# Blocks of the v table three ahead of their sums, and a store and a load of expert weights in two, in a two-layer PEER network

## The chip, the cores and the metric

The kernel runs on one core of one Trainium2 chip. What counts is the device time in microseconds (us) of one execution. The core has five engines with queues of instructions of their own: TensorE (PE; PEld is its weight load), VectorE (DVE), ScalarE (ACT), GpSimd (POOL) and SyncE (SP). SP issues most of the transfers, ACT the stores of two intermediate results, POOL the indirect gathers; 16 DMA engines carry them all.

## The reference, cut to what matters

The network has two layers. In each, three mixers (a state-space scan, differential attention, neighbourhood attention) are merged, and then comes a mixture of 16384 experts, each of which is one row of a table u and one row of a table v. For every token 8 heads choose 16 experts each:

```python
def peer_ffn(h, wq, subkeys, u_tab, v_tab):
    ...
        q = (hb @ wq).reshape(bn, PEER_CHUNK, PEER_HEADS, 2, PEER_DHALF)
        s = jnp.einsum('bchxd,hxnd->bchxn', q, subkeys).astype(jnp.float32)
        sv, si = lax.top_k(s, PEER_TOPK)
        ...
        eidx = jnp.take_along_axis(cidx, pos, axis=-1)
        g = jax.nn.softmax(best, axis=-1).astype(hb.dtype)
        act = jax.nn.gelu(jnp.einsum('bchkd,bcd->bchk', u_tab[eidx], hb))
        return jnp.einsum('bchk,bchkd->bcd', g * act, v_tab[eidx])
```

There are 512 tokens of 1024 channels and 256 context tokens; the last layer needs the tokens alone. All is float32.

## The kernel before, in words

The change lies in the expert part. The kernel computes it in two ways side by side. For some tokens (two tiles of 128 in layer 0, one in layer 1) it gathers the chosen rows of u and v: `gathered` lets POOL fetch 128 rows of 4 KB at a time into one of 5 buffers `grow` (512 KB), and DVE works each off (L1234 for u, L1242 for v). For the others (n = 512 tokens in layer 0, 384 in layer 1) it computes all 16384 experts densely, in 128 blocks of 128 experts, and multiplies each with a weight that is zero for an expert that wasn't chosen.

The dense way has two stages. In the **early stage** `early` multiplies the u blocks with the tokens, and ACT stores the activations of each block in DRAM (`actd`, L1258 and L1259). Meanwhile `route` finds the chosen experts and makes the weight tables: for each token group of 32 tokens PE sums a table `gst` (128 x 128 experts x 32 tokens, 2 MB), ACT evicts it (L1190) and stores it in DRAM (`gd<-gst`, L1193). There are 16 token groups in layer 0 and 12 in layer 1; the last one is ready at the very end of the early stage. In layer 0 a part of the gathers of u is also still under way there: twelve rows of it stand on DVE behind the early stage's last work.

Then come the **sums**, in `experts`. `block(i)` brings a block's operands: every eighth block the weights of the next eight blocks for all token groups (`gt<-gd`, 2 MB in layer 0, 1.5 MB in layer 1), the block's activations (`act`, 256 or 192 KB), and the v table's block (`raw`, 512 KB). DVE multiplies w = act * gt (L1278). Products are made in three passes of a shorter format, so `split` cuts w into wh (ACT, L61) and wl (DVE, L62), and `chunk` cuts raw into hiv (ACT, L61) and lov (DVE, L62). `sums` issues the matmuls wh x hiv (L1288), wh x lov (L1289) and wl x hiv (L1291), which add up in PSUM over all blocks. The last 4 blocks (LAST) are all made first and then summed tile by tile. Beside the sums run the rest of the gathers and what finishes their tokens (`beside`).

The order on each engine is that in which the program writes its instructions, by generators that take turns; an engine goes through its queue in that order, and each instruction waits for its operands and for its buffer. The pools of the early stage are closed ahead of the sums, and the sums' pools lie in the same memory: the first tiles of the sums also wait until what lay there has been read or stored. Below, hi and lo belong to u blocks, hiv and lov to v blocks.

Of the kernel before, what the change touches and what calls it, by code (L numbers as in the profile page):

```python
# [50 lines left out]
class Net:  # L51
# [1044 lines left out]
    def route(self, l, sv, si, p, picks=None, at=None):  # L1096


        nc, v = self.nc, self.nc.vector
# [29 lines left out]
        def lookup(out, x, against, table, op):  # L1129
            for h in range(0, 8, 2):  # L1130
                sh = [128, 2, 16, 16]
                eq = p.tile(sh, F32, name="eq")
                v.tensor_tensor(eq, x[:, 16 * h:16 * h + 32].rearrange("p (h k) -> p h k", h=2).unsqueeze(3).to_broadcast(sh),
                                against[:, None, None, :].to_broadcast(sh), op=op)
                v.tensor_tensor(eq, eq, table[:, h:h + 2][:, :, None, :].to_broadcast(sh), op=ALU.mult)
                v.tensor_reduce(out[:, 16 * h:16 * h + 32].rearrange("p (h k) -> p h k", h=2), eq, axis=AX.X, op=ALU.add)
                yield 1.30
# [44 lines left out]
        def table(b, t0, st, oj, og, ol):  # L1182
            for q in range(0, 8, 4):
                ps = self.ps1("mm")
                for z in range(4):
                    o = ps[:, 128 * z:128 * z + 128]
                    a, y = divmod(q + z, 2)
                    nc.tensor.matmul(o, oj[:, a, :, y], og[:, a, :, y], start=True, stop=False)
                    nc.tensor.matmul(o, oj[:, a, :, y], ol[:, a, :, y], start=False, stop=True)
                nc.scalar.activation(st[:, :, t0 + q:t0 + q + 4].rearrange("p i t -> p t i"),  # L1190
                                     ps.rearrange("p (t i) -> p t i", t=4), AF.Copy, scale=1.0 / GSCALE)
            if t0 == 24:
                nc.scalar.dma_start(self.gd[l][at + b], st)  # L1193

        last = None
        for b in range(4):
            st = p.tile([128, 128, 32], F32, name="gst", tag="gst")
            for t0 in range(0, 32, 8):
                t = 32 * b + t0
                oi, oj, og = [p.tile(sh, F16, name=n, bufs=3) for n in ("oi", "oj", "og")]  # L1200
                v.tensor_tensor(oj, iota, over(ij[:, 1], t), op=ALU.is_equal)
                v.tensor_tensor(oi, iota, over(ij[:, 0], t), op=ALU.is_equal)
                v.tensor_tensor(og, oi, over(gh, t), op=ALU.mult)
                v.tensor_tensor(oi, oi, over(gl, t), op=ALU.mult)
                if last is not None:
                    table(*last)
                last = b, t0, st, oj, og, oi
                yield 2.40
        table(*last)

    def gathered(self, l, halves, rows, picks, p):
# [50 lines left out]
    def experts(self, l, n, p, ends, fill, cost):  # L1262


        nc, v = self.nc, self.nc.vector
        nh = n // 128
        stay = [self.ps2() for _ in range(nh)]
        parts = {}
        spent = 0.0

        def block(i):
            if i % 8 == 0:
                self.gt = p.tile([128, 4 * nh, 8, 32], F32, name="gt")
                self.dma(self.gt, self.gd[l][16 - 4 * nh:, :, i:i + 8].rearrange("b j i t -> j b i t"))
            act = p.tile([128, n], F32, name="act", bufs=3)
            self.dma(act, self.actd[l][i, :, :n])
            w = p.tile([128, n], F32, name="w")
            v.tensor_mul(w.rearrange("p (b t) -> p b t", t=32), act.rearrange("p (b t) -> p b t", t=32), self.gt[:, :, i % 8])  # L1278
            wh, wl = [p.tile([128, n], F32R, name=a, bufs=LAST + 2) for a in ("wh", "wl")]
            self.split(w, wh, wl)  # L1280
            parts[i] = (wh, wl, *self.chunk(self.a["peer_v"][l, i], "v"))

        def sums(i, x):
            ps, t = stay[x], slice(128 * x, 128 * x + 128)
            cs = [slice(512 * s, 512 * s + 512) for s in range(2)]
            wh, wl, vh, vl = parts[i]
            for c in cs:
                nc.tensor.matmul(ps[:, c], wh[:, t], vh[:, c], start=i == 0, stop=False)  # L1288
                nc.tensor.matmul(ps[:, c], wh[:, t], vl[:, c], start=False, stop=False)  # L1289
            for c in cs:  # L1290
                m = nc.tensor.matmul(ps[:, c], wl[:, t], vh[:, c], start=False, stop=i == 127)  # L1291
            return m

        marks = [None] * AHEAD
        for i in range(128 - LAST):
            block(i)
            for x in range(nh):
                m = sums(i, x)
            marks.append(m)
            self.pace = marks.pop(0)  # L1300
            while fill is not None and spent < cost * (i + 1) / (128 - LAST):
                c = next(fill, None)
                if c is None:
                    fill = None
                else:
                    spent += c
        for _ in fill or ():
            pass
        for i in range(128 - LAST, 128):
            block(i)  # L1310
        for x in range(nh):
            for i in range(128 - LAST, 128):
                sums(i, x)
            ends(x, stay[x])
# [273 lines left out]
```

## Time and profile before

| | |
|---|---|
| three runs | 4790.73, 4791.86, 4794.95 us (median 4791.86) |
| profiled execution: its own time | 4793.69 us |
| profiled execution: its span, first to last instruction | 4791.9 us |
| mean granted clock of PE, as a share of full speed | 0.961 |
| PE busy | 4438.4 us (93%) |
| DVE busy | 3780.0 us (79%) |
| ACT busy | 1858.3 us (39%) |
| POOL busy | 1129.2 us (24%) |
| moved by the DMA engines | 1209.93 MB, 252 GB/s over the span |

The profile is one execution. Its times count from the span's start. An engine is busy while it computes; issuing a transfer and waiting don't count. A granted clock (PEclk) of 1.00 is 2.4 GHz, one of 0.50 is 1.2 GHz. Behind an instruction of a timeline, square brackets name the idle time of its engine ahead of it and what released it; an engine's name with a q behind it (ACTq, SPq) is the issuing of a transfer. SP's transfers run on the queue q1, ACT's on q10, POOL's gathers on q0.

### The profile page before, as it was taken

What the parts mean: (1) busy time and instruction counts of PE and PEld (TensorE: products, weight loads), DVE (VectorE), ACT (ScalarE), POOL (GpSimd) and SP (SyncE); (2) the same over time, 40 slices, a digit from 0 to 9 for tenths busy, and PEclk for the clock granted to TensorE, in tenths of its full rate; (3) what the DMA queues carried; (4) which work ended last, traced back from release to release, by engine and by line L of the source; (5) the groups of instructions that cost most, each with busy time, mean ns of one, the idle gap of its engine ahead of it and who ended that gap; (6) DMA issues with size and microseconds to landing.
All of it is one profiled execution on the core that took longest, in us unless ns stands there. A gap on an engine that the chain in (4) does not pass through costs nothing. (4 is left out here: it accounts for less than half of the span.)

```text
span 4791.9 us, 68877 instructions
## 1 busy us (share of the span) xinstructions
PE 4438.4 (93%) x24197; PEld 3715.9 (78%) x24197; DVE 3780.0 (79%) x8710; ACT 1858.3 (39%) x3079; POOL 1129.2 (24%) x772
## 2 busy tenths in 40 slices
PE   8998998889989999879999997999889999989998
PEld 4787886677767778658888876877789899968887
DVE  8377985668888999987787763877555899968887
ACT  3244454443222445443222223445333355533333
POOL 0000000000555355534433300000000133325552
PEclk9999998899999999989999998999899999999999
DMA  7453435654899789999999945442444599999997
GB/s 245 152 146 103 145 119 173 222 185 148 305 337 322 246 320 341 348 352 378 358 343 352 344 175 171 142 142 89 166 149 138 191 333 356 341 331 381 377 375 260
DMA packets 461397, 1209.93 MB, mean 252 GB/s; under 512 B 47530, under 2 KB 181754, under 8 KB 457466
## 3 DMA queue, kind: packets, MB, share of 16 engines
q1 hardware_dynamic: 309562, 685.37, 42.0%
q0 software_dynamic: 110592, 402.70, 23.0%
q10 hardware_dynamic: 40896, 117.46, 6.3%
q8 instruction: 190, 3.11, 0.3%
q14 instruction: 157, 1.29, 0.1%
HBM read 1026.30 MB, written 179.04 MB: 252 GB/s over the span
## 5 line engine op out<-in xcount | busy, mean ns | idle before, releaser
L1220 POOL DMA_INDIRECT grow<-in_u_rows,pick x384 | 514.9, 1341 | 2900.1 <-DVE cand L1104 1179.5
L61 ACT CAST hi<-raw 128x1024 fp32r<-128x1024 f32 x490 | 513.0, 1052 | 876.1 <-PE s L71 602.2
L62 DVE TENSOR_TENSOR lo<-raw,hi 128x1024 fp32r<-128x1024 f32 x490 | 596.4, 1220 | 284.7 <-ACT hi L61 279.9
L72 PE MATMUL s<-h2h,lo 128*128 128x512 f32 (+1 forms) x2048 | 760.7, 372 | 49.6 <-DVE lo L62 49.2
L70 PE MATMUL s<-h2h,hi 128*128 128x512 f32 (+1 forms) x2048 | 769.7, 376 | 9.3 <-ACT eact L1258 9.0
L1220 POOL DMA_INDIRECT grow<-in_v_rows,pick x384 | 614.1, 1599 | 693.8 <-PE stay L1291 248.4
L71 PE MATMUL s<-h2l,hi 128*128 128x512 f32 (+1 forms) x2048 | 759.1, 371 | 0.0
L1288 PE MATMUL stay<-hiv,wh 128*128 128x512 f32 x1792 | 708.5, 396 | 47.5 <-ACT hiv L61 47.5
L1289 PE MATMUL stay<-lov,wh 128*128 128x512 f32 x1792 | 708.6, 395 | 0.0
L1242 DVE SCALAR_TENSOR_TENSOR row<-grow,gw,row 128x1024 f32<-128x1024 f32 x381 | 488.3, 1282 | 98.9 <-DMA grow<-in_v_rows,pick 95.8
L1291 PE MATMUL stay<-hiv,wl 128*128 128x512 f32 x1792 | 562.7, 395 | 0.0
L1234 DVE SCALAR_TENSOR_TENSOR grow<-grow,row 128x1024 f32<-128x1024 f32 x384 | 463.3, 1220 | 98.0 <-DMA grow<-in_u_rows,pick 92.4
L72 PEld LDWEIGHTS s<-h2h,lo 128*128 128x128 f32 x2048 | 389.8, 190 | 108.7 <-DVE lo L62 64.2
L61 ACT CAST wh<-w 128x512 fp32r<-128x512 f32 (+1 forms) x256 | 145.5, 569 | 773.3 <-DVE w L1278 369.5
L1288 PEld LDWEIGHTS stay<-hiv,wh 128*128 128x128 f32 x1792 | 338.5, 189 | 126.5 <-ACT hiv L61 47.9
L70 PEld LDWEIGHTS s<-h2h,hi 128*128 128x128 f32 x2048 | 390.4, 191 | 55.3 <-ACT eact L1258 13.4
L71 PEld LDWEIGHTS s<-h2l,hi 128*128 128x128 f32 x2048 | 390.3, 191 | 43.1
L1289 PEld LDWEIGHTS stay<-lov,wh 128*128 128x128 f32 x1792 | 338.4, 189 | 80.3 <-DVE lov L62 1.3
L1291 PEld LDWEIGHTS stay<-hiv,wl 128*128 128x128 f32 x1792 | 338.1, 189 | 78.9
L62 DVE TENSOR_TENSOR lov<-raw,hiv 128x1024 fp32r<-128x1024 f32 x256 | 312.4, 1220 | 6.5 <-ACT hiv L61 5.0
L61 ACT CAST hiv<-raw 128x1024 fp32r<-128x1024 f32 x256 | 268.3, 1049 | 64.1 <-DMA raw<-in_peer_v 62.2
L1278 DVE TENSOR_TENSOR w<-act,gt 128x512 f32<-128x512 f32 (+1 forms) x256 | 158.8, 621 | 102.9 <-DMA act<-actd 101.4
(424 smaller groups left out, 8759.6 us busy)
## 6 DMA issues: line engine op xcount, KB each, us to landing
raw<-in_peer_u SPq DMA_DIRECT2D x256, 512.0 KB
raw<-in_peer_v SPq DMA_DIRECT2D x256, 512.0 KB
gd<-gst ACTq DMA_DIRECT2D x28, 2048.0 KB
raw<-in_w_in SPq DMA_DIRECT2D x88, 512.0 KB
actd<-eact ACTq DMA_DIRECT2D x128, 256.0 KB
gt<-gd SPq DMA_DIRECT2D x16, 2048.0 KB
act<-actd SPq DMA_DIRECT2D x128, 256.0 KB
adaw<-in_ada_w SPq DMA_DIRECT2D x48, 512.0 KB
```

Of the source, the lines that this page charges most:

```text
L61: self.nc.scalar.copy(hi, x)
L62: self.nc.vector.tensor_sub(lo, x, hi.bitcast(F32))
L70: mm(ps, lh, rh, start=start and k == 0, stop=False)
L71: mm(ps, lh, rl, start=False, stop=False)
L72: mm(ps, ll, rh, start=False, stop=stop and k == n - 1)
L1220: d = nc.gpsimd.indirect_dma_start(out=t, out_offset=None, in_=self.a[table], in_offset=bass.IndirectOffsetOnAxis(ap=picks[y][0][:, j:j + ...
L1234: v.scalar_tensor_tensor(t, t, 1.0, h, op0=ALU.mult, op1=ALU.mult, accum_out=u[:, j:j + 1])
L1242: v.scalar_tensor_tensor(h, t, w[:, j:j + 1], h, op0=ALU.mult, op1=ALU.add)
L1278: v.tensor_mul(w.rearrange("p (b t) -> p b t", t=32), act.rearrange("p (b t) -> p b t", t=32), self.gt[:, :, i % 8])
L1288: nc.tensor.matmul(ps[:, c], wh[:, t], vh[:, c], start=i == 0, stop=False)
L1289: nc.tensor.matmul(ps[:, c], wh[:, t], vl[:, c], start=False, stop=False)
L1291: m = nc.tensor.matmul(ps[:, c], wl[:, t], vh[:, c], start=False, stop=i == 127)
```

## The change

Three things change, for both layers. The store of the last token group's table is cut at expert block 8: first the weights of the first 8 blocks (128 KB), then those of the other 120 (1.92 MB). The first load of gt is cut too: first all token groups but the last (15 in layer 0, 11 in layer 1), then the last one (128 KB). And the blocks of v are loaded and split three blocks ahead: those of blocks 0, 1 and 2 before the first block, and block i + 3's at the head of `block(i)`.

```diff
--- before.py
+++ after.py
@@ -1190,7 +1190,10 @@
                 nc.scalar.activation(st[:, :, t0 + q:t0 + q + 4].rearrange("p i t -> p t i"),
                                      ps.rearrange("p (t i) -> p t i", t=4), AF.Copy, scale=1.0 / GSCALE)
             if t0 == 24:
-                nc.scalar.dma_start(self.gd[l][at + b], st)
+
+                cuts = (0, 8, 128) if at + b == 15 else (0, 128)
+                for i, j in zip(cuts, cuts[1:]):
+                    nc.scalar.dma_start(self.gd[l][at + b, :, i:j], st[:, i:j])
 
         last = None
         for b in range(4):
@@ -1268,17 +1271,29 @@
         parts = {}
         spent = 0.0
 
+        def table(i):
+            if i < 128:
+                tables[i] = self.chunk(self.a["peer_v"][l, i], "v")
+
+
+        tables = {}
+        for i in range(3):
+            table(i)
+
         def block(i):
+            table(i + 3)
             if i % 8 == 0:
                 self.gt = p.tile([128, 4 * nh, 8, 32], F32, name="gt")
-                self.dma(self.gt, self.gd[l][16 - 4 * nh:, :, i:i + 8].rearrange("b j i t -> j b i t"))
+                cuts = (0, 4 * nh - 1, 4 * nh) if i == 0 else (0, 4 * nh)
+                for b, e in zip(cuts, cuts[1:]):
+                    self.dma(self.gt[:, b:e], self.gd[l][16 - 4 * nh + b:16 - 4 * nh + e, :, i:i + 8].rearrange("b j i t -> j b i t"))
             act = p.tile([128, n], F32, name="act", bufs=3)
             self.dma(act, self.actd[l][i, :, :n])
             w = p.tile([128, n], F32, name="w")
             v.tensor_mul(w.rearrange("p (b t) -> p b t", t=32), act.rearrange("p (b t) -> p b t", t=32), self.gt[:, :, i % 8])
             wh, wl = [p.tile([128, n], F32R, name=a, bufs=LAST + 2) for a in ("wh", "wl")]
             self.split(w, wh, wl)
-            parts[i] = (wh, wl, *self.chunk(self.a["peer_v"][l, i], "v"))
+            parts[i] = (wh, wl, *tables.pop(i))
 
         def sums(i, x):
             ps, t = stay[x], slice(128 * x, 128 * x + 128)
```

What this moves shows on three engines. In the rows that follow, brackets name what an instruction waits for: DMAHW (a transfer of SP's or ACT's, the digit is its semaphore), DMASW (a gather of POOL's), or an engine.

SP, beginning of layer 0's sums, before:

```order
L58 DMA raw<-in_peer_u 128x1024 [waits DMAHW4_49,DMAHW0_49,DVE_49]
L58 DMA raw<-in_peer_u 128x1024 [waits DMAHW7_49,DMAHW2_49,DVE_49]
L58 DMA gt<-gd_107 128x16x256 [waits DMAHW4_49,DMAHW3_49,DMAHW7_49,DVE_49,Activation_49]
L58 DMA act<-actd_109 128x512 [waits DMAHW5_49,Activation_49]
L58 DMA raw<-in_peer_v 128x1024 [waits DMAHW6_49,DMAHW1_49]
L58 DMA act<-actd_109 128x512
```

and with the change:

```order
L58 DMA raw<-in_peer_u 128x1024 [waits DMAHW4_49,DMAHW0_49,DVE_49]
L58 DMA raw<-in_peer_u 128x1024 [waits DMAHW7_49,DMAHW2_49,DVE_49]
L58 DMA raw<-in_peer_v 128x1024 [waits DMAHW5_49,DMAHW1_49,DVE_49]
L58 DMA raw<-in_peer_v 128x1024 [waits DMAHW6_49,DMAHW3_49,DVE_49]
L58 DMA raw<-in_peer_v 128x1024 [waits DMAHW7_49,DVE_49]
L58 DMA raw<-in_peer_v 128x1024 [waits DMAHW0_49,DVE_49]
L58 DMA gt<-gd_107 128x15x256 [waits DMAHW1_49,DMAHW3_49,DVE_49,Activation_49]
L58 DMA gt<-gd_107 128x256 [waits DMAHW3_49,DMAHW2_49]
L58 DMA act<-actd_109 128x512 [waits DMAHW4_49,Activation_49]
L58 DMA raw<-in_peer_v 128x1024
L58 DMA act<-actd_109 128x512 [waits DMAHW5_49]
```

Four loads of v and 15 groups of gt now stand ahead; the last group's load and the first act follow them.

DVE at the same place, before:

```order
L1234 SCALAR_TENSOR_TENSOR grow,gu<-grow,row_9271 128x1024 [waits DMASW3_49,DVE_49]
L1234 SCALAR_TENSOR_TENSOR grow,gu<-grow,row_9271 128x1024 [waits DMASW4_49,DVE_49]
L1234 SCALAR_TENSOR_TENSOR grow,gu<-grow,row_9271 128x1024 [waits DMASW5_49,DVE_49]
L1278 TENSOR_TENSOR w<-act,gt 128x512 [waits DMAHW4_49,DMAHW5_49,DMAHW3_49,Activation_49]
L62 TENSOR_TENSOR wl<-w,wh 128x512 [waits PE_49,Activation_49]
L1278 TENSOR_TENSOR w<-act,gt 128x512 [waits DMAHW7_49]
L62 TENSOR_TENSOR lov<-raw,hiv 128x1024 [waits DMAHW6_49,Activation_49]
```

and with the change (line numbers are 3 and 15 higher):

```order
L1237 SCALAR_TENSOR_TENSOR grow,gu<-grow,row_9271 128x1024 [waits DMASW3_49,DVE_49]
L1237 SCALAR_TENSOR_TENSOR grow,gu<-grow,row_9271 128x1024 [waits DMASW4_49,DVE_49]
L1237 SCALAR_TENSOR_TENSOR grow,gu<-grow,row_9271 128x1024 [waits DMASW5_49,DVE_49]
L62 TENSOR_TENSOR lov<-raw,hiv 128x1024 [waits DMAHW5_49,PE_49,Activation_49]
L62 TENSOR_TENSOR lov<-raw,hiv 128x1024 [waits DMAHW6_49,Activation_49]
L62 TENSOR_TENSOR lov<-raw,hiv 128x1024 [waits DMAHW7_49,Activation_49]
L62 TENSOR_TENSOR lov<-raw,hiv 128x1024 [waits DMAHW0_49,Activation_49]
L1293 TENSOR_TENSOR w<-act,gt 128x512 [waits DMAHW3_49,DMAHW4_49,DMAHW2_49,DMAHW1_49]
L62 TENSOR_TENSOR wl<-w,wh 128x512 [waits PE_49,Activation_49]
```

The rows of the gather stay ahead; four lov have come between the last of them and the first w.

ACT, beginning of layer 1's sums, before:

```order
L1259 DMA actd_110<-eact 128x384 [waits Activation_49]
L1190 ACTIVATE gst<-mm 128x4x128 [waits PE_49] x2
L1193 DMA gd_108<-gst 128x4096 [waits Activation_49]
L61 CAST wh<-w 128x384 [waits DMAHW1_49,DVE_49]
L61 CAST hiv<-raw 128x1024 [waits DMAHW4_49]
L61 CAST wh<-w 128x384 [waits DVE_49]
```

and with the change:

```order
L1262 DMA actd_110<-eact 128x384 [waits Activation_49]
L1190 ACTIVATE gst<-mm 128x4x128 [waits PE_49] x2
L1196 DMA gd_108<-gst 128x256 [waits Activation_49]
L1196 DMA gd_108<-gst 128x3840
L61 CAST hiv<-raw 128x1024 [waits DMAHW5_49,DVE_49]
L61 CAST hiv<-raw 128x1024 [waits DMAHW6_49,DVE_49]
L61 CAST hiv<-raw 128x1024 [waits DMAHW7_49,DVE_49]
L61 CAST hiv<-raw 128x1024 [waits DMAHW0_49]
L61 CAST wh<-w 128x384 [waits DMAHW4_49,DMAHW3_49,DVE_49]
L61 CAST hiv<-raw 128x1024 [waits DMAHW4_49]
```

The store is in two, and four casts hiv stand ahead of the first wh, which now waits for two transfers besides w.

## Rows read from the trace of the kernel before

**Rows 1.** The page, part 5: the sums' first matmul line.

```profile
L1288 PE MATMUL stay<-hiv,wh 128*128 128x512 f32 x1792 | 708.5, 396 | 47.5 <-ACT hiv L61 47.5
```

**Rows 2.** Windows over both stretches of sums: busy us of each engine.

```profile
2152.37:2862.00 709.63, 709.63 (x3050) 574.99 (x3051) 545.39 (x659) 204.32 (x262) 244.18 (x186) 1.00 0.91 329
4241.17:4778.90 537.73, 537.69 (x2304) 435.06 (x2304) 449.98 (x574) 191.76 (x261) 238.43 (x141) 1.00 0.97 357
```

**Rows 3.** Timeline of PE, both joints; in brackets the idle time before.

```profile
2125.37 0.22 PE L1189 MATMUL mm<-oi,oj 128*128 128x128 f16 x1
2152.37 1.65 PE L1288 MATMUL stay<-hiv,wh 128*128 128x512 f32 x3 [26.78 <-ACT hiv L61]
...
4220.19 0.22 PE L1189 MATMUL mm<-oi,oj 128*128 128x128 f16 x1
4241.17 1.22 PE L1288 MATMUL stay<-hiv,wh 128*128 128x512 f32 x2 [20.76 <-ACT hiv L61]
```

**Rows 4.** Timeline of ACT, joint of layer 1.

```profile
4222.31 0.33 ACTq L1193 DMA_DIRECT2D gd<-gst  x1
4239.43 0.51 ACT L61 CAST wh<-w 128x384 fp32r<-128x384 f32 x1 [17.14 <-DVE w L1278]
4240.07 1.05 ACT L61 CAST hiv<-raw 128x1024 fp32r<-128x1024 f32 x1
```

**Rows 5.** Timeline of SP, joint of layer 1.

```profile
4228.65 0.38 SPq L58 DMA_DIRECT2D gt<-gd  x1
```

**Rows 6.** Timeline of DVE, joint of layer 1.

```profile
4238.84 0.56 DVE L1278 TENSOR_TENSOR w<-act,gt 128x384 f32<-128x384 f32 x1 [21.26 <-DMA act<-actd]
```

**Rows 7.** Windows ahead of the two joints.

```profile
2099.00:2106.00 7.00, 6.39 (x50) 4.91 (x50) 7.00 (x12) 3.62 (x4) 3.46 (x4) 1.00 0.84 252
2106.00:2113.00 7.00, 6.50 (x39) 5.02 (x38) 7.00 (x13) 2.35 (x4) 3.45 (x3) 1.00 0.98 400
...
2120.00:2127.00 7.00, 5.59 (x36) 4.32 (x35) 7.00 (x12) 2.44 (x4) 4.82 (x3) 1.00 0.69 201
...
4216.00:4222.00 6.00, 4.41 (x36) 4.08 (x34) 1.57 (x4) 3.21 (x5) 0.00 (x0) 1.00 0.11 37
```

**Rows 8.** Timeline of DVE, its last instruction.

```profile
4786.89 1.23 DVE L1334 TENSOR_TENSOR raw<-raw 128x1024 f32<-128x1024 f32 x1
```

**Rows 9.** Timeline of DVE, beginning of layer 0's sums.

```profile
2152.61 1.22 DVE L62 TENSOR_TENSOR lov<-raw,hiv 128x1024 fp32r<-128x1024 f32 x1
2153.75 0.69 DVE L62 TENSOR_TENSOR wl<-w,wh 128x512 fp32r<-128x512 f32 x1
```

**Rows 10.** Timeline of ACT, joint of layer 0.

```profile
2127.18 0.33 ACTq L1193 DMA_DIRECT2D gd<-gst  x1
2150.75 0.62 ACT L61 CAST wh<-w 128x512 fp32r<-128x512 f32 x1 [23.60 <-DVE w L1278]
```

**Rows 11.** Timeline of SP, joint of layer 0.

```profile
2137.15 0.38 SPq L58 DMA_DIRECT2D gt<-gd  x1
```

**Rows 12.** Timeline of DVE, joint of layer 0.

```profile
2146.24 1.23 DVE L1234 SCALAR_TENSOR_TENSOR grow<-grow,row 128x1024 f32<-128x1024 f32 x1 [3.20 <-DMA grow<-in_u_rows,pick]
2150.02 0.69 DVE L1278 TENSOR_TENSOR w<-act,gt 128x512 f32<-128x512 f32 x1 [2.55 <-DMA act<-actd]
```

**Rows 13.** Windows inside the joint of layer 0.

```profile
2127.00:2137.00 10.00, 0.00 (x0) 0.00 (x0) 2.75 (x6) 0.15 (x1) 4.27 (x4) 0.60 0.99 375
2137.00:2150.00 13.00, 0.00 (x0) 0.00 (x0) 6.17 (x10) 0.00 (x0) 1.10 (x1) 0.50 1.04 382
```

**Rows 14.** DMA queues, 2127 to 2137, then 2137 to 2146.2.

```profile
q10 hardware_dynamic: 288, 2.36, 57.2%
q0 software_dynamic: 383, 1.39, 41.6%
...
q0 software_dynamic: 559, 2.01, 54.6%
q1 hardware_dynamic: 1480, 1.52, 48.8%
```

## The prediction

> **What bounds the kernel now.** I read the page's costliest groups first. PE is busy for 93% of the span, and the group that carries the expert sums has 47.5 us of idle time ahead of it, all of it put down to the cast hiv [rows 1]. Then the windows over both stretches of sums: PE is busy for 709.63 of 709.63 us in layer 0 and for 537.69 of 537.73 us in layer 1 [rows 2]. So inside a stretch nothing can be won, and the 47.5 us must lie ahead of them. The timeline of PE shows where: between the last matmul of the weight tables and the first of the sums it stands for 26.78 us in layer 0 and for 20.76 us in layer 1 [rows 3]. I call these two places the joints. What starts the sums earlier moves everything behind them by as much; the end of layer 0's sums leads into layer 1, and the last matmul (4778.90) into the tail. So the change is worth what it takes off the two joints.
>
> **Layer 1's joint, as it is.** ACT issues the store of the last weight table at 4222.31 [rows 4]. SP's gt load, which reads it back, goes at 4228.65 [rows 5]: the store took 6.34 us. The product w starts at 4238.84, after 21.26 us in which DVE had nothing else to do [rows 6]: gt and act took 10.2 us. Then come wh at 4239.43 and hiv at 4240.07 [rows 4], and PE at 4241.17 [rows 3].
>
> **What the change does there.** The last token group leaves in two stores, the first with the 8 first experts only (128 KB). The 11 groups stored long before are loaded without waiting for it, and so are v blocks 0 to 3: on SP they wait for buffers of the early stage only (first and third excerpt of the change). Ahead of this joint the DMA engines are busy for a share of 0.11 at 37 GB/s [rows 7], so these loads find room. What stays in the chain is: small store, small gt load, w, wh.
>
> - *Small store.* No row shows a 128 KB store. Above lies the line through two others: 2.1 MB in 6.34 us, and 0.52 MB of output in at most 3.8 us (DVE's last result at 4786.89 + 1.23 = 4788.12 [rows 8], span's end 4791.9). That is 1.6 us per MB, so at most 3.2 us for 0.13 MB. Below lie its bytes alone, 0.3 us. I take 2.0, a little over the middle, since the 0.52 MB row is the nearer one: it lands at 4224.3. The Trainium skill ("DMA: Bandwidth & Descriptors", Anatomy of one DMA) gives each DMA about 2.0 us of fixed time besides its bytes, which speaks against cutting; by it the small store would take an estimated 2.3 us, and the sum would be 0.3 us worse. No row here shows that fixed time by itself.
> - *gt and act loads.* At best 2 us, as the small store: 4226.3. At worst the 6.34 us of the whole store, which runs beside them, behind a small store of 3.2: 4231.9. I take 4230.1, near the upper end, because the 1.92 MB of the other store are under way until about 4229 (4222.7 + 6.34).
> - *wh* now lies where the old table lay, and waits for the second store too: 4229 to 4230. It costs nothing more if the loads come at 4230.1.
> - *v blocks.* Four casts hiv of 1.05 us [rows 4] fill ACT from 4223.0, and DVE makes four lov behind them, at a pitch of 1.14 (2153.75 less 2152.61 [rows 9]). They end at about 4228.6, just ahead of w: covered by the store. Without that cover they would add up to 4.56 us.
> - From w's start to wh 0.59, from there to wh's end 0.64 with the hand-over [rows 4, 6]: PE starts at 4230.1 + 1.2 = **4231.3, 9.8 us earlier**. Bounds: 4229.9 (four lov first, then w at 4228.6: -11.3) and 4233.1 (-8.0).
>
> **Layer 0's joint, as it is.** The store goes at 2127.18 [rows 10], gt's load at 2137.15 [rows 11]. This joint has other work: twelve rows of the gather wait on DVE, the last of which starts at 2146.24 after 3.20 us of waiting for its data, and w follows at 2150.02 [rows 12]. PE starts 6.13 us after that last gather landed. The DMA engines are full: share 0.99 at 375 GB/s, then 1.04 at 382 [rows 13].
>
> **What the change does there.**
> - *DVE's order.* Four lov now stand between the last gather row and w (the second excerpt of the change). From the landing: 1.23 for the gather row, 4 x 1.14 for the lov, 0.73 from w's start to wh and 0.62 for wh [rows 9, 10, 12]: 7.2 us instead of 6.13, **+1.07**. The casts hiv come from ACT, which has nothing else then (wh waited 23.60 us [rows 10]).
> - *The act load* still waits for the whole store, to about 2137.5; but 2 MB of gt no longer stand before it, so it lands before the gather does, and costs nothing.
> - *The last gather.* More bytes now ask for the engines before it: 2.1 MB of v, 2.1 of gt and 0.26 of act, 4.46 MB, where SP's queue had moved 1.52 MB from 2137 until the gather landed [rows 14]: 2.94 MB more. Room was there for 0.52 MB (one v block; 2099 to 2106, 252 GB/s) and (376 - 201) GB/s x 7 us = 1.22 MB (2120 to 2127) [rows 7]. The other 1.2 MB take 3.2 us at 376 GB/s. But the gathers have a queue of their own and hold about half of the engines' time beside the others: 41.6% to the store's 57.2%, then 54.6% to the loads' 48.8% [rows 14]. So about half of it comes first: 1.5 us. Ends: the gather lands right behind the one before it, whose row ended at 2143.1 (3.20 of waiting less 0.08 before the next could start: -3.1), or all 2.94 MB come ahead of it (+7.8).
> - Together **+2.5 us**, between -2.0 and +8.9.
>
> **What costs nothing.** Two more stores to issue on ACT and two more loads on SP, 0.33 and 0.38 us each [rows 4, 5], lie where both engines stand idle in the joint. POOL's and PE's instructions stay as they are. In the sums each v block is made three blocks earlier and w is not; DVE is busy for 545 of 710 us there [rows 2], so w keeps a lead of four to five blocks at the beginning, where it had six. In the joints PE's granted clock falls to 0.50, its lower level of 1.2 GHz [rows 13]; both joints stay over 10 us long, and over the first 10 us of layer 0's the mean was 0.60 already, so I count the slow first matmuls the same as before.
>
> **The sum.** -9.8 + 2.5 = **-7.3 us**. The profiled execution took 4793.69 us for a span of 4791.9; it would take 4786.4. It is 1.83 above the median of the runs, 4791.86, so the median should be **4784.5**. About 0.2% (9.6 us) is what a measurement of this kernel can tell from no change: under 4782.3 is faster, over 4801.4 slower.
>
> **The rivals.**
> - *A, both joints gain.* With gt and v out of the way by 2127, the last gather of layer 0 has the engines to itself and lands right behind its forerunner: -2.0 there, -11.8 in all, **4780.1**. For it: before, 1.52 MB of loads ran beside that gather [rows 14]. Against it: the room ahead was not enough for them, by 1.2 MB.
> - *B, the loads go ahead of the gathers.* SP issues 2.1 MB of v and 1.97 MB of gt as soon as buffers of the early stage come free (an estimated 2099 to 2122, by the DVE and ACT instructions that they wait for), in front of the last gathers, and the gathers' rows stand in DVE's queue ahead of w and among the lo that the early stage needs. DVE is busy for 7.00 of 7.00 us in each of the windows ahead of layer 0's joint, with the engines at a share of 0.98 between [rows 7]; so a gather that comes late there stops it, and PE soon after. Price: 4.1 MB at 0.38 MB per us, 10.8 us on the last gather, 1.07 for the lov, and 1.57 MB (three v blocks that find no room) in the early stage, 4.1 us: +16.0 in layer 0, with -9.8 in layer 1 +6.2, **4798**. It decides from 9.8 us lost in layer 0 on; over 0.2% slower takes 19.4, twice the stall in the early stage. Against it: the gathers hold their 41.6% beside a store [rows 14].
> - *C, given back in the sums.* A shorter lead and DMA engines at 0.91 and 0.97 [rows 2] let PE wait for v or w in the first blocks: no change, **4791.9**. Against it: a block keeps PE for 709.63 / 128 = 5.5 us, and its four lov are made ahead.
> - *D, the cut works only in part.* The 128 KB, or act and wh, wait until the whole store has landed and its loads have followed: -8.0 in layer 1 and +2.5 in layer 0, -5.5, **4786.4**. What would make it so: the small load goes in short pieces beside the store's long ones (2.36 MB of the store in 288 packets, against 1480 packets for 1.52 MB of loads [rows 14]), and takes turns with them. The Trainium skill ("DMA: Bandwidth & Descriptors", Queues, rings and completion order) says that a DMA engine goes round the queues packet by packet. By that rule the short pieces wait for a long one at each turn; the trace agrees that gathers and store ran side by side, and shows no 128 KB load.
>
> **How the numbers follow.** Forecast 0.45, A 0.32, D 0.09, C 0.06, B 0.08, of which 0.05 lie over 0.2%. The forecast, D, C and the rest of B are within 0.2%: 0.45 + 0.09 + 0.06 + 0.03 = 0.63. A is faster: 0.32. The range goes from both lower bounds together (-13.3, rounded down: 4778.5) to 4791.0 (-8.0 in layer 1, +7.1 in layer 0, a little short of the upper bound of 8.9); it leaves out C and most of B.
>
> **What would show it.** The sums of layer 1 start near 4231 less what layer 0 gained, with a joint of about 11 us instead of 20.76; layer 0's joint is 29.3 instead of 26.78, with its last gather row at 2147.7 and four lov between it and w. It is wrong if layer 0's joint is shorter than before (A), if PE stands still in a stretch of sums (C), or if DVE waits for gathers before 2127 (B).

## The result, and the profile after

The changed kernel takes 4814.33 us (median of five runs, 4810.12 to 4824.30) against 4791.86 us of the kernel before (five runs, 4788.13 to 4794.95): a ratio of 1.0055, with an interval of 1.0042 to 1.0068. It is **slower by 22.5 us**. The profiled execution of the changed kernel took 4810.12 us, with a span of 4808.4.

The page's costliest groups show in one line where it went: the matmuls with wl, which never waited before (first line, from the page before the change), now wait 18 us for DVE.

```profile
L1291 PE MATMUL stay<-hiv,wl 128*128 128x512 f32 x1792 | 562.7, 395 | 0.0
...
L1303 PE MATMUL stay<-hiv,wh 128*128 128x512 f32 x1792 | 715.4, 399 | 44.1 <-ACT wh L61 44.1
L1306 PE MATMUL stay<-hiv,wl 128*128 128x512 f32 x1792 | 568.3, 398 | 18.1 <-DVE wl L62 18.0
```

The windows over the two stretches of sums, and over 100 us in the middle of the second (window: length, then busy us and instructions of PE, PEld, DVE, ACT and POOL, PEclk, DMA share, GB/s), place it in layer 1:

```profile
2151.30:2864.00 712.70, 712.70 (x3050) 573.57 (x3051) 543.23 (x656) 200.93 (x259) 239.63 (x186) 1.00 0.89 324
4231.48:4795.40 563.92, 545.83 (x2304) 438.71 (x2304) 445.73 (x571) 187.12 (x258) 235.51 (x141) 0.99 0.93 339
...
4600.00:4700.00 100.00, 94.65 (x393) 75.55 (x392) 76.55 (x92) 32.05 (x44) 47.52 (x27) 0.97 0.96 348
```

Layer 0's stretch is still full. Layer 1's takes 563.92 us instead of 537.73 [rows 2]: 18.1 us in which PE stands still, and 8.1 us (545.83 less 537.69) that the same 2304 matmuls take longer. The timeline of PE gives both joints, and eight stalls of over 0.5 us, 35 to 38 us apart (eight blocks) or twice that, of which two stand here:

```profile
2151.30 0.79 PE L1303 MATMUL stay<-hiv,wh 128*128 128x512 f32 x1 [28.71 <-ACT wh L61]
...
4231.48 0.80 PE L1303 MATMUL stay<-hiv,wh 128*128 128x512 f32 x1 [15.38 <-ACT wh L61]
...
4412.96 0.72 PE L1306 MATMUL stay<-hiv,wl 128*128 128x512 f32 x2 [2.56 <-DVE wl L62]
...
4736.22 1.22 PE L1306 MATMUL stay<-hiv,wl 128*128 128x512 f32 x2 [2.65 <-DVE wl L62]
```

The 8.1 us have two parts. About 2 to 3 us belong to the execution: layer 0's 3050 matmuls, which never wait, took 712.70 us here and 709.63 before [rows 2], both at a clock of 1.00, and in cut_only, an experiment below without a stall, layer 1's 2304 took 540.66 us. (From 2250 to 2750, 2144 matmuls ran here and in before_four_w, which makes no v ahead, 2154 before and in start3; so it isn't the change.) The rest goes with the granted clock, 0.99 over the stretch and 0.97 over the 100 us above, where it had been 1.00. Behind four of the eight stalls (1.76, 3.08, 2.27 and 2.65 us long) it fell towards its lower level, to a mean of 0.83 to 0.85 in windows of 10 us; behind the other four, one of them of 2.56 us, it stayed at 1.00. cut_only's sums, then the windows around a stall of 2.56 us and one of 3.08:

```profile
4233.60:4774.30 540.70, 540.66 (x2304) 433.63 (x2304) 450.36 (x574) 191.63 (x261) 236.54 (x141) 1.00 0.97 356
```

```profile
4410.00:4420.00 10.00, 7.44 (x32) 5.73 (x31) 9.32 (x11) 3.85 (x6) 4.32 (x3) 1.00 0.74 270
4620.00:4630.00 10.00, 6.92 (x25) 5.24 (x24) 5.07 (x7) 2.60 (x4) 1.66 (x1) 0.85 0.79 285
```

Measured from the store of the last table to the first matmul of the sums, the joints went from 25.19 us to 27.14 in layer 0 and from 18.86 to 13.49 in layer 1 [rows 3, 4, 10]. So +1.95 - 5.37 + 26.2 = **+22.8 us** for the joints and layer 1's sums in these two executions. That this comes so near the 22.5 us between the medians is partly chance: the two executions lie 16.5 us apart, as the rest of the program took 6.3 us less in this one, and 35 runs of the kernel before in one later series spread over 4784 to 4802.

**What stalls the sums.** One stall, in the timelines of SP and DVE of the changed kernel:

```profile
4389.63 0.47 SPq L58 DMA_DIRECT2D gt<-gd  x1
4392.05 3.60 SPq L58 DMA_DIRECT2D raw<-in_peer_v  x2
4395.69 1.61 SPq L58 DMA_DIRECT2D act<-actd  x2
...
4410.68 0.56 DVE L1293 TENSOR_TENSOR w<-act,gt 128x384 f32<-128x384 f32 x1 [7.66 <-DMA act<-actd]
4411.16 1.28 DVE L1245 SCALAR_TENSOR_TENSOR row<-grow,gw,row 128x1024 f32<-128x1024 f32 x1
4412.35 0.55 DVE L62 TENSOR_TENSOR wl<-w,wh 128x384 fp32r<-128x384 f32 x1
```

and the same place in the kernel before, where blocks 40 to 43 are made:

```profile
4396.97 0.58 SPq L58 DMA_DIRECT2D gt<-gd  x1
4399.85 0.89 SPq L58 DMA_DIRECT2D act<-actd  x1
4400.82 2.15 SPq L58 DMA_DIRECT2D raw<-in_peer_v  x2
...
4411.92 0.56 DVE L1278 TENSOR_TENSOR w<-act,gt 128x384 f32<-128x384 f32 x1 [1.57 <-DMA act<-actd]
4412.39 1.28 DVE L1242 SCALAR_TENSOR_TENSOR row<-grow,gw,row 128x1024 f32<-128x1024 f32 x1
4413.59 0.55 DVE L62 TENSOR_TENSOR wl<-w,wh 128x384 fp32r<-128x384 f32 x1
```

In both, SP issues gt for block 48 on while act of block 43 is still to be loaded. Before, that act goes out next; its w starts 15.0 us after gt was issued. With the change, two v loads (1 MB) stand between, and w starts 21.1 us after gt: **6.1 us later**. This place is among the wider ones: over layer 1's gt loads for blocks 32 to 120, the w whose act comes first behind gt starts 14.4 to 18.1 us after it before and 19.5 to 22.3 us with the change, 4.6 us later on the mean. Behind that w stand a gather row and the wl of the block before it, 42, and this wl is what PE waits for at 4412.96. The program's listing shows all of this. SP's queue in layer 1, before and with the change (in brackets the block, counted from 0):

```text
before: L58 DMA gt<-gd_108 128x12x256         after: L58 DMA gt<-gd_108 128x12x256
        L58 DMA act<-actd_110 128x384  (43)          L58 DMA raw<-in_peer_v 128x1024
        L58 DMA raw<-in_peer_v 128x1024              L58 DMA raw<-in_peer_v 128x1024
        L58 DMA raw<-in_peer_v 128x1024              L58 DMA act<-actd_110 128x384  (43)
```

and DVE's, whose order is the same in both kernels (43025 belongs to block 42, 42993 to block 41; those of blocks 43 and 42 follow in the same order):

```text
L1293 TENSOR_TENSOR w_43025<-act_43023,gt_42948 128x384
L1245 SCALAR_TENSOR_TENSOR row2_32792<-grow_42904,gw_42115,row2_32792 128x1024
L62 TENSOR_TENSOR wl_42993<-w_42990,wh_42992 128x384
```

So the order of the loads is not the written one: a gt load stands up to five blocks ahead of its place, and with the change every one of layer 1 from block 16 on has two v loads and then act behind it. In layer 0 some gt loads have two and some one; PE doesn't stall there, with 5.5 us to a block instead of 4.2 and the engines at 0.89 instead of 0.93.

**The joint of layer 1.** The loads of gt (the first and the last of the two), the two stores, and w:

```profile
L58 SPq DMA_DIRECT2D gt<-gd x2: 333/358/382, 4215.9 to 4224.7; - x2
```

```profile
4217.99 0.89 ACTq L1196 DMA_DIRECT2D gd<-gst  x2
...
4230.32 0.56 DVE L1293 TENSOR_TENSOR w<-act,gt 128x384 f32<-128x384 f32 x1 [5.64 <-DMA act<-actd]
```

The small store went at 4217.99, and the gt load that waits for it at 4224.7: 6.7 us for 128 KB. The load of the 11 other groups went at 4215.9 only, behind four v loads that had waited for buffers, and its 1.4 MB were under way at the same time. The DMA queues show what that did (packets, MB, share of the engines' time). From 4220 to 4222 the gt load's queue q1 held 94.2% of the engines' time and the store's queue q10 moved nothing; most of the store's 128 KB came only from 4222 on. Why the two didn't take turns there, no run shows. From 4224 to 4228 the queues do: the gt loads (q1, in pieces of 1 KB) and the large store (q10) moved about as many packets each, so that the loads got 0.11 MB through beside 1.58 MB of the store.

```profile
q1 hardware_dynamic: 516, 0.53, 94.2%
...
q10 hardware_dynamic: 106, 1.58, 92.4%
q1 hardware_dynamic: 104, 0.11, 7.4%
```

**The joint of layer 0.** The last gather row starts 20.06 us after the store (2124.16), 1.00 later than before; four lov and w follow as foreseen:

```profile
2144.22 1.22 DVE L1237 SCALAR_TENSOR_TENSOR grow<-grow,row 128x1024 f32<-128x1024 f32 x1 [0.50 <-DMA grow<-in_u_rows,pick]
...
2149.91 0.68 DVE L1293 TENSOR_TENSOR w<-act,gt 128x512 f32<-128x512 f32 x1
```

The gathers came a little into the early stage's way: ahead of the store DVE waits for them three times after 2100, 2.7 us in all, and before the change not at all. It cost nothing that shows, as layer 0's first table store and its last lie 484.5 us apart in both executions.

### The profile page after: what moved, and what is told of

It reads as the page before. It is cut to its first block, busy times and chain, and to the rows that moved or that the text cites. A ratio compares the mean times of both kernels' runs of the same rounds, so it can differ in the third digit from the quotient of the medians.

```text
span 4808.4 us, 68864 instructions
## 1 busy us (share of the span) xinstructions
PE 4443.6 (92%) x24197; PEld 3714.5 (77%) x24197; DVE 3781.9 (79%) x8710; ACT 1855.3 (39%) x3079; POOL 1118.5 (23%) x772
## 3 DMA queue, kind: packets, MB, share of 16 engines
q0 software_dynamic: 110592, 402.70, 22.8%
## 5 line engine op out<-in xcount | busy, mean ns | idle before, releaser
L1306 PE MATMUL stay<-hiv,wl 128*128 128x512 f32 x1792 | 568.3, 398 | 18.1 <-DVE wl L62 18.0
```

## The experiments

Two theories stood at first. The **lead theory** takes up the shorter lead of the prediction's rival C: v blocks made ahead take buffers, so that w runs ahead by less. The **order theory**, later called the queue theory: act stands behind v loads that are needed later.

**start3.** v ahead at the beginning alone:

```diff
         def block(i):
-            table(i + 3)
...
+            if i not in tables:
+                table(i)
             parts[i] = (wh, wl, *tables.pop(i))
```

> The changed kernel, but only blocks 0 to 2 of v are made ahead; from block 3 on each block makes its own v block behind its w, as before the change. The lead theory (v three blocks ahead takes three of the seven v buffers, so that w, which stands behind the v block in every queue, leads the sums by four blocks instead of six, and the gt loads of layer 1 no longer fit in): no stall over 0.5 us inside layer 1's sums, joints as with the change (layer 0 about 2 us longer from store to sums, layer 1 about 5 us shorter), so about 4788 us (4785 to 4791). The order theory (act and gt stand behind v loads that are needed later) says the same here. If instead the earlier start itself is paid back, because layer 1's sums are bound by their transfers: stalls stay, 4805 to 4815.

Measured: 4788.75 us against 4793.76 (ratio 0.9989, 0.9980 to 0.9998). PE has no stall in layer 1's sums, which take 537.6 us; the joints are 25.04 and 11.12 us (layer 0's 0.15 us shorter than before, not 2 longer as expected; layer 1's 7.7 shorter). The loss comes from what goes on during the sums, not from starting them earlier.

**ten_buffers_l1.** More buffers for v in layer 1:

```diff
-self.stream(ROWS, 2, LAST + 3)
+self.stream(ROWS, 2, LAST + 3 + 3 * l)
```

> The changed kernel with ten instead of seven buffers for hiv and lov in layer 1; the order of all instructions stays as with the change. The lead theory: w leads by six again, the stalls of layer 1's sums go, about 4788 us. The order theory: act and gt stand behind later v loads as before, the stalls stay, 4810 to 4820.

Measured: 4797.28 against 4793.76 (1.0003, 0.9995 to 1.0012); no stalls (sums 538.1 us), but layer 1's joint is 17.17 us. It seemed to speak for the lead theory. Its premise was wrong: with more buffers the listing has act directly behind gt again in layer 1, so lead and order changed together, and the run doesn't tell them apart. Its joint is longer because both parts of the first gt load went out at 4238.13 only, 6.6 us after the store; why the load of the 11 groups waited, the run doesn't show.

**before_four_w.** The lead cut in the old kernel:

```diff
-wh, wl = [p.tile([128, n], F32R, name=a, bufs=LAST + 2) for a in ("wh", "wl")]
+wh, wl = [p.tile([128, n], F32R, name=a, bufs=LAST) for a in ("wh", "wl")]
```

> The kernel before with four instead of six buffers for wh and wl, nothing else: w leads by four blocks and the order of transfers is the old one. The lead theory: layer 1's sums get stalls every eighth block as with the change, some 15 to 27 us in all, 4807 to 4819; layer 0's stay without. The order theory: no stalls, 4792.

Measured: 4794.63 against 4793.76 (1.0001, 0.9991 to 1.0010). PE waits 0.9 us for wl in all. Layer 1's sums take 540.0 us, of which PE is busy for 539.1: this is mostly the slower pace that cut_only's execution has too, and not waiting.

```profile
L1291 PE MATMUL stay<-hiv,wl 128*128 128x512 f32 x1792 | 564.9, 396 | 0.9 <-DVE wl L62 0.9
```

The lead theory's 15 to 27 us are not there. That alone doesn't refute it, since the lead that I had counted in buffers isn't reached anyway: in the kernel before, w of block 43 starts at 4411.92, when PE is at block (4411.92 - 4241.17) / 4.2 = 40.7, so 2.3 blocks ahead and not six.

**cut_only.** Store and load cut, no v ahead (each block makes its own, as before):

```diff
-            table(i + 3)
...
-            parts[i] = (wh, wl, *tables.pop(i))
+            parts[i] = (wh, wl, *self.chunk(self.a["peer_v"][l, i], "v"))
```

> Only the store and the first gt load are cut, no v block is made ahead. Lead theory and order theory: no stalls in the sums. The joints: in layer 1 the load of the 11 groups no longer stands behind four v loads in SP's queue, is done before the table is stored, and the small store meets idle engines: about 2 us for it instead of 6.6, joint 8 to 10 us shorter than before; in layer 0 no lov stands ahead of w, joint 0 to 3 us shorter. 4780 to 4784. If the cut itself is what stalls the sums: 4805 or more.

Measured: 4785.89 against 4793.76 (0.9982, 0.9972 to 0.9992). No stalls; the joints are 24.01 us (1.18 less than before) and 10.85 (8.01 less). The cut alone is a gain of 0.2%, a little short of what was expected. Its gt loads and stores in layer 1's joint:

```profile
L58 SPq DMA_DIRECT2D gt<-gd x2: 333/358/382, 4207.0 to 4224.5; - x2
```

```profile
4222.75 0.81 ACTq L1196 DMA_DIRECT2D gd<-gst  x2
```

With the 11 groups loaded from 4207.0 on, the small store takes 1.75 us (4222.75 to 4224.5) instead of 6.7. In start3, with three v loads ahead and the 11 groups at 4221.8, it took 4.45. So the later the load of the 11 groups goes out ahead of the store, the longer the small store takes.

**v_loads_ahead_of_before.** The old kernel, with the order of SP's loads alone as in the change:

```diff
+        def load(i):
+            if i < 128:
+                raws[i] = self.row()
+                self.dma(raws[i], self.a["peer_v"][l, i])
...
+            for j in range(0 if i == 0 else i + 3, i + 4):
+                load(j)
...
-            parts[i] = (wh, wl, *self.chunk(self.a["peer_v"][l, i], "v"))
+            vh, vl = [self.sp.tile([128, D], F32R, name=a, bufs=self.npart["v"]) for a in ("hiv", "lov")]
+            self.split(raws.pop(i), vh, vl)
+            parts[i] = (wh, wl, vh, vl)
```

> The kernel before, with the loads of the v blocks alone three ahead; hiv and lov are made where they were, from seven buffers, nothing is cut. On SP two v loads (1 MB) now stand between each later gt load of layer 1 and the act behind it, as with the change. The queue theory (that act comes late, since 1 MB of v goes ahead of it behind the 1.5 MB of gt, and w of that block with it): stalls every eighth block in layer 1's sums, the sums 15 to 27 us longer, 4805 to 4820. The lead theory (v made three ahead takes buffers, w leads by less): no stalls, 4788 to 4796.

Measured: 4822.77 against 4792.71 (1.0061, 1.0048 to 1.0074). Nothing is split ahead, nothing cut, and the whole loss is there, a little more than expected: layer 1's sums take 566.5 us.

```profile
L1302 PE MATMUL stay<-hiv,wl 128*128 128x512 f32 x1792 | 566.8, 398 | 19.1 <-DVE wl L62 19.1
```

```profile
4474.12 0.65 SPq L58 DMA_DIRECT2D gt<-gd  x1
4476.53 4.84 SPq L58 DMA_DIRECT2D raw<-in_peer_v  x2
4481.41 3.73 SPq L58 DMA_DIRECT2D act<-actd  x2
...
4496.03 0.56 DVE L1287 TENSOR_TENSOR w<-act,gt 128x384 f32<-128x384 f32 x1 [8.53 <-DMA act<-actd]
```

The same picture as with the change: gt, two v loads, act; w waits 8.53 us for act and starts 21.9 us after gt. The queue theory holds, the lead theory falls.

**acts_ahead_too.** The change, with act three blocks ahead as well, in six buffers:

```diff
-            act = p.tile([128, n], F32, name="act", bufs=3)
-            self.dma(act, self.actd[l][i, :, :n])
+            act = acts.pop(i)
...
+                acts[i] = p.tile([128, n], F32, name="act", bufs=6)
+                self.dma(acts[i], self.actd[l][i, :, :n])
...
+            if i:
+                fetch(i + 3)
             table(i + 3)
```

> The changed kernel with the act loads three blocks ahead too, in six buffers instead of three; v stays three ahead in seven buffers. Behind each gt load of layer 1 there are still two v loads, but the act behind them is one needed three blocks (12.6 us) later. The queue theory: no stalls over 0.5 us in layer 1's sums, 4786 to 4794. The lead theory: the v buffers are as few as with the change, the stalls stay, 4808 to 4820.

Measured: 4794.03 against 4792.71 (1.0001, 0.9992 to 1.0011). Two v loads still stand behind gt, and the buffers and the order of v are those of the change, but PE no longer waits. The gt load shown is that of block 56, and the act behind the two v loads is that of block 54, where the change has that of block 51 there:

```profile
L1316 PE MATMUL stay<-hiv,wl 128*128 128x512 f32 x1792 | 563.1, 395 | 0.0
```

```profile
4425.02 0.43 SPq L58 DMA_DIRECT2D gt<-gd  x1
4427.43 6.24 SPq L58 DMA_DIRECT2D raw<-in_peer_v  x2
4433.73 1.19 SPq L58 DMA_DIRECT2D act<-actd  x2
```

So the change is cured by giving the late load three blocks more. Its joints (24.86 and 12.79 us) are 6.4 us shorter than before, and its time isn't. In its profiled execution layer 0's first and last table store lie 492.5 us apart instead of 484.5, and DVE waits 5.8 us for gathers ahead of the last; but the other executions lie between 484.5 and 491.8, and its runs spread over 19 us, so where the gain went stays open.

**one_ahead.** The change, with one block instead of three (`table(i + 1)`, `range(1)`):

> The changed kernel with v one block ahead instead of three. One v load (0.5 MB) stands between gt and act in layer 1. The queue theory: act comes half as much later as with the change (1.5 to 2 us later than before); the w of that block had 1 to 1.5 blocks (4 to 6 us) to spare, so no stalls or a few under 1 us, 4786 to 4797. If the stalls grow in proportion to the bytes: half of the change's, 4800 to 4805.

Measured: 4789.06 against 4792.71 (0.9990, 0.9981 to 0.9998). Half the bytes behind gt, and PE waits 3.8 us in all, in two stalls; layer 1's sums take 542.3 us. The w behind gt starts 17.5 to 21.0 us after it (blocks 32 to 120), 2.9 us later than before on the mean, where the change has 4.6. So the delay is somewhat over half of the change's and the waiting a fifth (3.8 us against 18.1), which fits a block that has some time to spare. The two stalls, 2.2 and 1.6 us, are longer than the 1 us expected.

```profile
L1306 PE MATMUL stay<-hiv,wl 128*128 128x512 f32 x1792 | 563.2, 396 | 3.8 <-DVE wl L62 3.8
```

**start_one.** As start3, with block 0 alone ahead (`range(1)`):

> Store and gt load cut, and only block 0 of v made ahead, the rest as before. No v load behind gt, so no stalls. The load of the 11 groups goes earlier than with three or four v blocks ahead of it, so the small store of layer 1 takes 2 to 4 us instead of 6.6; in layer 0 one lov of 1.14 us stands ahead of w instead of four. About as cut_only: 4783 to 4790 (before at 4792 to 4794).

Measured: **4781.96 against 4792.71** (0.9979, 0.9969 to 0.9989), better than both kernels, though not to be told from cut_only (0.9982), which makes no block ahead. The joints are 24.67 and 9.64 us, and the sums have no stall:

```profile
4223.34 0.79 PE L1304 MATMUL stay<-hiv,wh 128*128 128x512 f32 x1 [11.53 <-ACT wh L61]
```

```profile
L1307 PE MATMUL stay<-hiv,wl 128*128 128x512 f32 x1792 | 562.7, 395 | 0.0
```

**gt_on_act_queue and start_one_gt_on_act.** Two runs that were to tell the place on the queue from the sum of bytes, with the same edit on the change and on start_one:

```diff
-                    self.dma(self.gt[:, b:e],
+                    (self.nc.sync if i == 0 else self.nc.scalar).dma_start(self.gt[:, b:e],
```

> The changed kernel with every gt load but the first issued by ACT, so that it runs on ACT's queue and act and v loads on SP's queue no longer stand behind it. The queue theory (act is late because gt and two v loads stand ahead of it on the one queue): the stalls of layer 1's sums go or shrink under 5 us in all, 4786 to 4797. If it is the sum of bytes that the engines can't carry at that moment, whichever queue they stand on: the stalls stay, 4805 to 4820.

> start_one with every gt load but the first on ACT's queue, as in gt_on_act_queue; no v load is ahead of its block any more. If the move of gt to a queue of its own is what made the stalls of gt_on_act_queue (three queues then share the engines, and act and v on SP's queue get less): stalls here too, 4800 to 4820. If it was the v loads ahead, as with the change: no stalls, 4779 to 4787, as start_one.

Measured: 4825.50 against 4793.81 (1.0060, 1.0046 to 1.0073), and 4810.35 against 4794.36 (1.0038, 1.0024 to 1.0052). The queue theory's number for the first was missed. The second shows why the first doesn't decide: moving gt to a queue of its own stalls PE by itself, 14.7 us of waiting for wl where start_one has none. The DMA queues from 4300 to 4700 (packets, MB, share of the engines' time), of start_one and then of start_one_gt_on_act:

```profile
q1 hardware_dynamic: 46332, 87.11, 61.7%
q0 software_dynamic: 16993, 61.88, 39.4%
```

```profile
q1 hardware_dynamic: 26097, 65.26, 43.4%
q0 software_dynamic: 16440, 59.83, 39.4%
q10 hardware_dynamic: 18054, 18.31, 13.7%
```

The gathers (q0) keep 39.4%; SP's queue, which now carries act and v alone, falls from 61.7 to 43.4%, and with q10 it moves 83.6 MB where q1 alone had moved 87.1. The Trainium skill ("DMA: Bandwidth & Descriptors", Queues, rings and completion order) has the engines go round the queues packet by packet. The trace of the changed kernel agrees for 4224 to 4228 in layer 1's joint (106 packets to 104), and not for 4220 to 4222, when the store's queue moved nothing. Whether gt on its own queue takes turns from act and v, or they move less only because PE stands still, and what of the stalls comes from another order of loads on SP, no run here separates.

## Why the prediction was wrong

It forecast 4784.5 us, no change that can be told; the kernel is 22.5 us slower, outside the range of 4778.5 to 4791.0.

- **The step that failed** is under "What costs nothing": "In the sums each v block is made three blocks earlier and w is not; ... so w keeps a lead of four to five blocks at the beginning". It counted a lead in blocks, looked only at DVE's free time, and costed the rest of the sums at nothing, and it took the order at the beginning of the sums for the order in all of them. The listing of SP's loads behind any gt load of layer 1 from the third on would have shown act moved from right behind gt to behind two v loads; the price of moving a load begins with the bytes that it puts in another's way, here 1 MB. Shown in its place: act, and with it w, comes 4.6 us later behind each gt load, PE waits 18.1 us for wl, and layer 1's sums take 26.2 us more. v_loads_ahead_of_before has this order alone and the whole loss; acts_ahead_too keeps it, with act three blocks earlier, and has no stall.
- **Rival C** named the place (PE waits in the sums, as transfers fill the engines) and bounded it wrongly, at the gain it could give back. It put the waiting in the first blocks; the first stall of over 0.5 us comes 181 us into layer 1's sums, and they recur with gt load after gt load and don't stop once the gain of the joints is used up. The lower clock behind some of them adds 5 to 6 us. Its shorter lead was not the cause: v_loads_ahead_of_before splits no block of v ahead and has the whole loss, and acts_ahead_too splits three ahead and has no stall.
- **Rivals A and B**, layer 0's joint shorter by 2.0 or longer by 16, didn't happen: it is 1.95 longer. B's sign was there, DVE waiting for gathers ahead of the joint, with 2.7 us and without B's price. The kernel became slower in another place.
- **Rival D** was right about layer 1's joint in its mechanism: the gt loads' short pieces and the large store took turns, 104 packets to 106 from 4224 to 4228. It priced that joint at -8.0; it is -5.4, as the small store was late besides.
- **Layer 1's joint**: forecast -9.8, measured -5.4. The mis-sized term is the small store: 2.0 us taken, 6.7 measured, beyond the bound of 3.2. The 2.0 itself was sound for engines that move nothing else (1.75 in cut_only). The 2.3 estimated by the Trainium skill, "DMA: Bandwidth & Descriptors", Anatomy of one DMA, whose fit is of transfers that GpSimd issues, would have been a little too long for this one of ACT's. What the term left out is the gt load of 11 groups, which four v loads had pushed to 4215.9, so that 1.4 MB stood in the store's way. The text had said that these loads "find room". The term behind it (gt and act loads, 5.8 us taken) measured 5.6: 4224.7 to 4230.32.
- **Layer 0's joint**: forecast +2.5, measured +1.95. The lov ahead of w cost 0.95 (7.08 us from the last gather row to the sums, 7.2 foreseen), and the gather landed 1.0 later (1.5 foreseen). The first step held: with four lov ahead, acts_ahead_too and gt_on_act_queue have 7.08 us too. The second isn't shown by one execution: from the store to the last gather row it is 19.06 us before and 20.06 with the change, but 17.8 in acts_ahead_too, which loads as much ahead, and 20.5 in cut_only, which loads no v ahead. That the sum came out so near is partly luck.
- **The tail, the two extra issues, the restart at the lower clock** held: from the last matmul to the end it is 13.0 us in both, ACT waits 8.05 us for w behind its second store in layer 1, and the first 50 us of layer 0's sums hold 205 matmuls in both.

## What to carry to other kernels

A load that is issued earlier is put ahead of something. Where the engines are full, look through the whole queue, not only at its beginning, for the load that now comes behind it, and at whom that one serves; its price begins with the bytes that it has been put behind, less the time that it has to spare, and is paid once per period. If a prefetch is to shorten a joint, make it for the joint alone: start3 and start_one have no stall in the sums. That it gains anything here isn't shown, as cut_only does as well without. And let the loads that open the way, here those of the groups already stored, go first.

## What the runs showed of the hardware that was not expected

Stalls of 1.7 to 3.1 us took more than themselves, but not each of them: behind four of eight the granted clock fell from 1.00 to 0.83 to 0.85 over 10 us, in all some 5 to 6 us, and the length of the stall alone didn't decide (one of 1.76 us is among the four, one of 2.56 us isn't). Two executions at a clock of 1.00 still differed, without waiting, by 0.4% in the pace of the same matmuls (3050 in 709.63 and in 712.70 us).

128 KB, stored on ACT's queue, took 1.75 us from issue to the load that waits for it with engines that moved nothing else, and 6.7 us beside a load of 1.4 MB in pieces of 1 KB on SP's queue, most of which went first.
